# ConvFFN up and gate chunks as 2x2 block products by Strassen's algorithm

## The chip, the cores and the metric

The kernel runs on one core of a Trainium2 chip, in one launch. The metric is the device time of one execution in microseconds (us). The engines are TensorE (PE; PEld is its weight load), VectorE (DVE), ScalarE (ACT), GpSimd (POOL) and SyncE (SP), which here issues most DMAs. Tiles live in SBUF, results of TensorE in PSUM.

## The reference

Two layers of a decoder trunk work on 592 tokens: 16 learned meta tokens, 64 sample tokens (8 sequences of 8) and 512 prompt tokens. Layer 0 has mLSTM and retention heads as its mixer, layer 1 HGRN2; behind each mixer stands a causal ConvFFN. The change touches the ConvFFN alone. With model width 1024, inner width 2816 and a convolution of three taps it is

```python
def conv_ffn(xn, w_in, conv_w, conv_b, w_out, buf):
    t = xn.shape[1]
    u, gate = jnp.split(xn @ w_in, 2, axis=-1)
    padded = jnp.concatenate([buf, u], axis=1)
    conv = conv_b + sum(padded[:, j:j + t] * conv_w[j] for j in range(3))
    h = jax.nn.silu(conv) * gate
    return h @ w_out, padded[:, t:]
# in each layer: x = x + conv_ffn(rms_norm(x, norm_ffn[layer]), ...)
```

All inputs and outputs are f32. Beside the tokens the mixers' states and the last two rows of `u` of each sequence are returned.

## The kernel before

Features lie on partitions, tokens on columns. The residual is 8 chunks `x[c]` of 128 features by 592 tokens. Every f32 matrix product is made of three products of fp32r operands, with each operand split into a rounded part `hi` and a rest `lo`: hi by hi, hi by lo, lo by hi. The residual is split after its gain, before the norm: `gained` makes `h` and `xl` of each chunk, and the factor 1 / rms of each token (`rb`, the same on all partitions) is multiplied in when a result is read out of PSUM.

Weights come in tiles of 128 x 8 x 128 (one output chunk of 128 features for all 1024 inputs, 512 KB). `weights` (lines 296 to 312) issues the DMA into a raw tile `wr` (two slots), ScalarE casts it to `wh` (line 308, three slots), VectorE subtracts to `wl` (line 310, three slots). `stream` (278 to 294) keeps two such tiles fetched ahead of the block at work.

In the ConvFFN there are 22 blocks `in_block(fc)` a layer, one for each chunk of 128 inner features. A block takes the up tile and the gate tile: `dense` (316 on) issues for each of 8 input chunks and 3 terms two matmuls, one for each half of the tokens (296 columns in layer 0, 288 and 290 in layer 1), first for up into one PSUM tile `dp`, then for gate into another. All matmuls are recorded under line 123. Then VectorE reads the results out of PSUM, multiplied by `rb`: up into `ub` (lines 514 and 524), gate into `gt` (line 491). Around `ub` GpSimd does the small copies of the convolution's state (517 to 526). The convolution is one ScalarE pass and two VectorE passes over `cv` (493, 495), then Silu (497), two products with the gate (501, 502) and the split of the result into `bh` and `bl` (505, 506). These are the operands of the output products.

The blocks stand in the order fc 0 to 7, the output products of chunks 0 to 6, fc 8 to 14, those of 7 to 13, fc 15 to 21, those of 14 to 21. VectorE adds the output products to the residual (line 424). Block 0 carries the norm of the residual as hooks: `norm_rows` and `norm_bcast` (274 copies `rb` out of PSUM) run while its products are made.

Other lines that the prediction uses for durations: 225 (squares on GpSimd), 1135 and 1209 (GpSimd in the HGRN2 mixer), 1230 (VectorE there), 1368 (the final norm's products on GpSimd). Each engine takes its instructions in the order that the framework's scheduler wrote down when the kernel was built; there is no reordering on the chip.

## Time and profile before

| | |
|---|---|
| time, median of 3 runs | 1633.36 us (1633.0 to 1635.6) |
| span of the profiled execution | 1633.1 us |
| TensorE busy | 1584.1 us, 13508 matmuls |
| VectorE busy | 938.8 us |
| ScalarE busy | 625.8 us |
| GpSimd busy | 204.2 us |
| ConvFFN of layer 0, inside (640 to 745 us) | 773 matmuls in 105.00 us |
| ConvFFN of layer 1, inside (1310 to 1440 us) | 981 matmuls in 130.00 us |

The time of an execution is taken on the device; the profile is one execution with the hardware profiler on, and all durations below come from that one. Busy times of an engine are sums over its instructions, as the profiler records them from start to end; successive instructions can overlap by a little, so that a start to the next start is shorter than the duration listed.

### The profile page before, as it was taken

To read this page: it belongs to the slowest core of one execution; us is meant where nothing else is said; L and a number is where in the kernel's file an instruction comes from. 1 tells how busy PE (TensorE), PEld (TensorE's weight loads), DVE (VectorE), ACT (ScalarE), POOL (GpSimd) and SP (SyncE) were. 2 spreads that over 40 slices of the span, in tenths; PEclk is the share of its full clock that TensorE was granted. 3 is DMA by queue.
4 is the path that set the end of the run, shared out by engine and by line. 5 is a ranking of instruction groups with operands and counts; after the bars stand their busy time and mean duration, and the time that the engine had idled before them with its cause. 6 is when DMAs were issued, how large, how long until landed. Compare 5 with 4: busy or idle time off the path is not lost. (4 is left out here: it accounts for less than half of the span.)

```text
span 1633.1 us, 32234 instructions
## 1 busy us (share of the span) xinstructions
PE 1584.1 (97%) x13508; PEld 1538.7 (94%) x13508; DVE 938.8 (57%) x1933; ACT 625.8 (38%) x1114; POOL 204.2 (13%) x402
## 2 busy tenths in 40 slices
PE   4999999999999999999999899999999999999997
PEld 4999999999999999999999798898999999999997
DVE  5576564757553454355546876766675535534565
ACT  3543434334331232233345466564443213322343
POOL 4000000000110110010002525333001101100102
PEclk9999999999999999999999999999999999999998
DMA  4334435433323222322422132223233232223244
GB/s 144 97 94 100 94 89 83 141 95 95 88 73 87 78 81 75 91 78 85 146 74 66 56 102 91 61 95 96 92 101 89 71 93 84 74 85 88 80 120 135
DMA packets 236049, 149.61 MB, mean 92 GB/s; under 512 B 7512, under 2 KB 227416, under 8 KB 235904
## 3 DMA queue, kind: packets, MB, share of 16 engines
q1 hardware_dynamic: 235904, 147.56, 31.9%
q8 instruction: 106, 1.74, 0.4%
q14 instruction: 39, 0.32, 0.1%
HBM read 132.89 MB, written 14.65 MB: 90 GB/s over the span
## 5 line engine op out<-in xcount | busy, mean ns | idle before, releaser
L123 PE MATMUL dp<-h,wh 128*128 128x296 f32 (+2 forms) x2176 | 477.8, 301 | 0.8 <-ACT v_c L661 0.5
L308 ACT CAST wh<-wr 128x1024 fp32r<-128x1024 f32 (+3 forms) x240 | 234.1, 978 | 625.2 <-PE dp L123 485.5
L123 PE MATMUL dp<-xl,wh 128*128 128x296 f32 (+2 forms) x2176 | 472.1, 298 | 0.0
L123 PE MATMUL dp<-h,wl 128*128 128x296 f32 (+2 forms) x2176 | 471.7, 298 | 0.0
L123 PEld LDWEIGHTS dp<-h,wh 128*128 128x128 f32 x2176 | 351.2, 189 | 4.3 <-issue 1.8
L123 PEld LDWEIGHTS dp<-h,wl 128*128 128x128 f32 x2176 | 352.1, 189 | 0.0
L123 PEld LDWEIGHTS dp<-xl,wh 128*128 128x128 f32 x2176 | 351.8, 189 | 0.0
L310 DVE TENSOR_TENSOR wl<-wr,wh 128x1024 fp32r<-128x1024 f32 (+3 forms) x240 | 273.8, 1141 | 76.3 <-ACT wh L308 73.0
L123 PE MATMUL dp<-bh,wh 128*128 128x296 f32 (+2 forms) x832 | 182.8, 300 | 2.0 <-DVE x L424 0.5
L123 PE MATMUL dp<-bh,wl 128*128 128x296 f32 (+2 forms) x832 | 179.7, 297 | 0.0
L123 PE MATMUL dp<-bl,wh 128*128 128x296 f32 (+2 forms) x832 | 179.5, 297 | 0.0
L424 DVE TENSOR_TENSOR x<-x,dp 128x592 f32<-128x592 f32 (+2 forms) x72 | 54.9, 763 | 153.1 <-PE dp L123 153.0
L123 PEld LDWEIGHTS dp<-bh,wh 128*128 128x128 f32 x832 | 134.0, 188 | 5.9 <-ACT wh L308 2.4
L491 DVE TENSOR_TENSOR gt<-dp,rb 128x592 f32<-128x592 f32 (+1 forms) x44 | 33.7, 767 | 179.9 <-PE dp L123 179.8
L123 PEld LDWEIGHTS dp<-bl,wh 128*128 128x128 f32 x832 | 134.4, 188 | 0.0
L123 PEld LDWEIGHTS dp<-bh,wl 128*128 128x128 f32 x832 | 134.2, 188 | 0.0
L123 PE MATMUL tp<-wh,h 128*128 128x256 f32 (+3 forms) x280 | 84.6, 303 | 19.0 <-ACT wh L308 11.8
L123 PE MATMUL tp<-wl,h 128*128 128x256 f32 (+3 forms) x280 | 81.2, 290 | 0.3 <-DVE wl L310 0.3
L123 PE MATMUL tp<-wh,xl 128*128 128x256 f32 (+3 forms) x280 | 79.7, 289 | 1.9 <-DVE xl L216 1.9
L495 DVE SCALAR_TENSOR_TENSOR cv<-ub,vec,cv 128x612 f32<-128x612 f32 (+1 forms) x88 | 74.1, 842 | 1.6
L123 PEld LDWEIGHTS tp<-wh,h 128*128 128x128 f32 (+1 forms) x280 | 52.3, 187 | 24.0 <-ACT wh L308 11.8
L497 ACT ACTIVATE cv<-cv 128x612 f32<-128x612 f32 (+1 forms) x44 | 31.1, 708 | 90.8 <-DVE cv L495 90.8
(425 smaller groups left out, 1933.8 us busy)
## 6 DMA issues: line engine op xcount, KB each, us to landing
wr<-in_w_ffn_in SPq DMA_DIRECT2D x88, 512.0 KB, 3.8
wr<-in_w_in_ab SPq DMA_DIRECT2D x32, 512.0 KB, 7.0
wr<-in_w_in_c SPq DMA_DIRECT2D x32, 512.0 KB, 4.1
wr<-in_w_ffn_out SPq DMA_DIRECT2D x32, 448.0 KB, 3.5
wr<-in_w_ffn_out SPq DMA_DIRECT2D x24, 512.0 KB, 3.8
x<-in_x SPq DMA_DIRECT2D x16, 296.0 KB, 5.1
out_H<-s_s SPq DMA_DIRECT2D x8, 576.0 KB, 2.9
wr<-in_w_out_ab SPq DMA_DIRECT2D x16, 256.0 KB, 2.9
```

The source lines that it names most:

```text
L123: T.matmul(out, lhsT=lhsT, rhs=rhs, **kw)
L308: S.copy(hi, raw)
L310: V.tensor_tensor(out=lo, in0=raw, in1=hi.bitcast(F32), op=ALU.subtract)
L424: V.tensor_tensor(out=x[oc][:, a:b], in0=x[oc][:, a:b], in1=p[:, off + a:off + b], op=ALU.add)
L491: V.tensor_tensor(out=gt[:, h0:], in0=pg[:, off + h0:off + NT], in1=rb[:, h0:], op=ALU.mult)
L495: V.scalar_tensor_tensor(out=cv[:, b0:612], in0=ub[:, b0 + j:612 + j], scalar=cw[j], in1=cv[:, b0:612], op0=ALU.mult, op1=ALU.add)
L497: S.activation(cv[:, b0:612], cv[:, b0:612], AF.Silu)
```

## The change

Blocks fc 0 and 1 of each layer stay as they were. From block 2 on (`NOLD = 2`) the up tile and the gate tile of a chunk are taken together as a 2x2 matrix of blocks: rows up and gate, columns the first and the second 4 input chunks, A11, A12 (up), A21, A22 (gate), each 128 x 4 x 128. The tokens are cut in two halves, so that the normed residual is a 2x2 matrix too: B11, B12 (first 4 chunks, first and second half), B21, B22. Strassen's algorithm in Winograd's form makes the four result blocks of seven block products in place of eight; each product is 4 input chunks by 3 terms, 12 matmuls of 296 columns (layer 0) or 290 (layer 1), so that a block has 84 matmuls where it had 96.

The weights' block sums are four GpSimd additions of 128 x 512 (lines 379 to 382: A21+A22, that plus A11, A21+A11 in place of A21, and the second sum plus A12). Split are now two full tiles, one tile of two sums, and a half tile: 3.5 tiles a block where 2 were. `Split` makes each when it is asked for, and `ahead_step` asks for one of the next block's between two products. Raw tiles have a third slot (`alt`).

The operands of the tokens are made once a layer, while block 1 runs. `prepare` (608 to 633): ScalarE applies the gain, GpSimd multiplies by 1 / rms (613), and B11 (negated) and B21/B22 are split by ScalarE and VectorE. `differences` (634 to 639) makes the T blocks on GpSimd from these in 16 operations of 296 columns. `split_differences` (641 to 650) splits the T blocks, into the slots of `h` and `xl`, which the old form reads until block 1 is done.

Results in a block (`strassen_block`, 652 on): the seven products go into PSUM banks a, c (one tile `ac`), b (`sb`) and d (`sd`), in the order B11, B21, T2, T1, T3, T4, B22. Bank a accumulates over three of them, and ScalarE copies it out to SBUF after each (673, 688, 693). VectorE makes `ub` and `gt` as subtractions with one operand in PSUM (680, 685 and 700 for `ub`, 694 and 697 for `gt`). From there on `activate` (582 to 600) is what the old block had: 586 is the first step of the convolution, 588 the two on VectorE, 590 Silu, 597 the cast to `bh`.

```diff
-    # A block is (load, body): load() emits the weights' DMA and their split, body(w) is a generator.
-    def stream(blocks):
-        ahead = []
-        todo = iter(blocks)
-
...
-    def weights(*views):
-        """views: DRAM [128, k, n]; hi/lo f32r tiles of the same shape"""
-        out = []
-        for v in views:
-            k = v[0].shape[1]
-            n = sum(a.shape[2] for a in v)
-            raw = wp.tile([128, k, n], F32, name="wr", tag="wr", bufs=2)
-            o = 0
-            for a in v:
-                ld.dma_start(out=raw[:, :, o:o + a.shape[2]], in_=a)
-                o += a.shape[2]
-            hi = wp.tile([128, k, n], F32R, name="wh", tag="wh", bufs=3)
-            S.copy(hi, raw)
-            lo = wp.tile([128, k, n], F32R, name="wl", tag="wl", bufs=3)
-            V.tensor_tensor(out=lo, in0=raw, in1=hi.bitcast(F32), op=ALU.subtract)
-            out.append((hi, lo))
-        return out
...
+    class Split:
+        def __init__(self, k, n, src):
+            self.k, self.n, self.src, self.made = k, n, src, None
+
+        def get(self):
+            if self.made is None:
+                src = self.src() if callable(self.src) else self.src
+                hi = wp.tile([128, self.k, self.n], F32R, name="wh", tag="wh", bufs=3)
+                S.copy(hi, src)
+                lo = wp.tile([128, self.k, self.n], F32R, name="wl", tag="wl", bufs=3)
+                V.tensor_tensor(out=lo, in0=src, in1=hi.bitcast(F32), op=ALU.subtract)
+                self.made = (hi, lo)
+            return self.made
...
+
+    def ahead_step():
+
+        if ahead:
+            for sp in ahead[0][0] or ():
+                if sp.made is None:
+                    sp.get()
+                    return
...
+        fetch()
+        while ahead:
+            w, body = ahead.pop(0)
+            fetch()
+            for sp in w or ():
+                if not isinstance(w, Quadrants):
+                    sp.get()
+            n = 0
+            for i, (nw, _) in enumerate(ahead):
+                if isinstance(nw, Quadrants):
+                    if n == 0:
+                        nw.add()
+                        if not isinstance(w, Quadrants):
+                            nw[0].get()
+                            nw[1].get()
+                    break
+                if n >= 2 or isinstance(w, Quadrants):
+                    break
+                for sp in nw or ():
+                    sp.get()
+                    n += 1
+            yield from body(w)
+
...
+    turn = [0]
+
+    def quadrants(v1, v2):
+
+
+        r1, r2 = (raw_weights([v], (turn[0] + i) % 3 == 2) for i, v in enumerate((v1, v2)))
+        turn[0] += 2
+        env = {}
+
+        def sums():
+            s12 = tp.tile([128, 2, 4, 128], F32, name="s12", tag="ve", bufs=2)
+            s4 = tp.tile([128, 4, 128], F32, name="s4", tag="nums", bufs=2)
+            a11, a12, a21, a22 = r1[:, 0:4, :], r1[:, 4:8, :], r2[:, 0:4, :], r2[:, 4:8, :]
+            G.tensor_tensor(out=s12[:, 1], in0=a21, in1=a22, op=ALU.add)
+            G.tensor_tensor(out=s12[:, 0], in0=s12[:, 1], in1=a11, op=ALU.add)
+            G.tensor_tensor(out=a21, in0=a21, in1=a11, op=ALU.add)
+            G.tensor_tensor(out=s4, in0=s12[:, 0], in1=a12, op=ALU.add)
+            env.update(s12=s12.rearrange("p a k n -> p (a k) n"), s4=s4)
+
+        q = Quadrants([Split(8, 128, r1), Split(8, 128, lambda: env["s12"]), Split(8, 128, r2),
+                       Split(4, 128, lambda: env["s4"])])
+        q.sums = sums
+        return q
...
+        def prepare(c):
+
+            g = vec[:, V_NFFN + 8 * l + c:V_NFFN + 8 * l + c + 1]
+            x_ = xn[c] = ap.tile([128, NT], F32, name=f"xn{c}", tag=f"b{'hl'[c % 2]}{4 + c // 2}")
+            S.activation(x_, x[c], AF.Copy, scale=g)
+            G.tensor_tensor(out=x_, in0=x_, in1=state["rb"], op=ALU.mult)
+            if c < 4:
+                if c % 2 == 0:
+                    for i in "hl":
+                        ops["1", i, c // 2] = tp.tile([128, 2, 296], F32R, name=f"b11{i}", tag="gate", bufs=4)
+                hi, lo = (ops["1", i, c // 2][:, c % 2, 0:n] for i in "hl")
+                S.activation(hi, x_[:, h1], AF.Copy, scale=-1.0)
+                V.scalar_tensor_tensor(out=lo, in0=x_[:, h1], scalar=-1.0, in1=hi.bitcast(F32), op0=ALU.mult,
+                                       op1=ALU.subtract)
+                ops["B11", c] = (hi, lo)
+            else:
+                if c % 2 == 0:
+                    ops["2", "h", c // 2] = ap.tile([128, 2, 592], F32R, name="b2h", tag="v", bufs=2)
+                    ops["2", "l", c // 2] = tp.tile([128, 2, 592], F32R, name="b2l", tag="st", bufs=2)
+                hi, lo = (ops["2", i, c // 2][:, c % 2, 0:2 * n] for i in "hl")
+                S.copy(hi, x_[:, a0:NT])
+                V.tensor_tensor(out=lo, in0=x_[:, a0:NT], in1=hi.bitcast(F32), op=ALU.subtract)
+                ops["B21", c - 4] = (hi[:, 0:n], lo[:, 0:n])
+                ops["B22", c - 4] = (hi[:, n:2 * n], lo[:, n:2 * n])
+
+        def differences(c):
+
+            p, q = xn[c], xn[c + 4]
+            G.tensor_tensor(out=p[:, h1], in0=p[:, h1], in1=p[:, h2], op=ALU.subtract)
+            G.tensor_tensor(out=p[:, h2], in0=p[:, h2], in1=q[:, h2], op=ALU.subtract)
+            G.tensor_tensor(out=q[:, h2], in0=p[:, h1], in1=q[:, h2], op=ALU.add)
+            G.tensor_tensor(out=q[:, h1], in0=q[:, h2], in1=q[:, h1], op=ALU.subtract)
+
+        def split_differences():
+            for c in (4, 5, 6, 7, 0, 1, 2, 3):
+                hi = xslot(c, "h", F32R)
+                lo = ap.tile([128, NT], F32R, name=f"xl{c}", tag=f"xl{c}")
+                S.copy(hi[:, 0:2 * n], xn[c][:, a0:NT])
+                V.tensor_tensor(out=lo[:, 0:2 * n], in0=xn[c][:, a0:NT], in1=hi[:, 0:2 * n].bitcast(F32),
+                                op=ALU.subtract)
+                a, b = ("T1", "T3") if c < 4 else ("T4", "T2")
+                ops[a, c % 4] = (hi[:, 0:n], lo[:, 0:n])
+                ops[b, c % 4] = (hi[:, n:2 * n], lo[:, n:2 * n])
...
+            def product(out, split, k0, op, start, stop):
+                hi, lo = split.get()
+                for k in range(4):
+                    xh, xl = ops[op, k]
+                    for i, (ww, xx) in enumerate(((hi, xh), (hi, xl), (lo, xh))):
+                        matmul(out, lhsT=ww[:, k0 + k, :], rhs=xx, start=start and k == 0 and i == 0,
+                               stop=stop and k == 3 and i == 2, skip_group_check=True)
+                    if k % 2:
...
+            def body(w):
+                w.add()
+                w[0].get()
+                w[1].get()
+                ac = mm("ac")
+                a, c = ac[:, 0:n], ac[:, 512:512 + n]
+                cs = tmp("cs", 592)
+                s1, u2, u3 = cs[:, 0:n], cs[:, 296:296 + n], cs[:, 0:n]
+                yield from product(a, w[0], 0, "B11", True, True)
+                S.copy(s1, a)
+                w[2].get()
+                b = px("sb")[:, 0:n]
+                yield from product(b, w[0], 4, "B21", True, True)
+
+                ub, gt = tmp("ub", 614), tmp("gt")
+                ubs = ub[:, 0:100].rearrange("p (s i) -> p s i", i=10)
+                V.tensor_tensor(out=ubs[:, s0:, 2:10], in0=b[:, h0 - a0:80 - a0].rearrange("p (s i) -> p s i", i=8),
+                                in1=s1[:, h0 - a0:80 - a0].rearrange("p (s i) -> p s i", i=8), op=ALU.subtract)
+                if l == 1:
+                    V.tensor_tensor(out=ub[:, 100:102], in0=b[:, 2:4], in1=s1[:, 2:4], op=ALU.subtract)
+                m = a0 + n - P0
+                V.tensor_tensor(out=ub[:, 102:102 + m], in0=b[:, P0 - a0:n], in1=s1[:, P0 - a0:n], op=ALU.subtract)
+                up_edges(fc, ub)
+                yield from product(a, w[1], 0, "T2", False, True)
+                S.copy(u2, a)
+                w[3].get()
+                yield from product(c, w[1], 4, "T1", True, True)
+                ahead_step()
+                yield from product(a, w[2], 0, "T3", False, True)
+                S.copy(u3, a)
+                V.tensor_tensor(out=gt[:, h2], in0=u3, in1=c, op=ALU.subtract)
+                d = px("sd")[:, 0:n]
+                yield from product(d, w[2], 4, "T4", True, True)
+                V.tensor_tensor(out=gt[:, h1], in0=u3, in1=d, op=ALU.subtract)
+                ahead_step()
+                yield from product(c, w[3], 0, "B22", False, True)
+                V.tensor_tensor(out=ub[:, 102 + m:614], in0=c, in1=u2, op=ALU.subtract)
+                up_state(fc, ub)
+                activate(fc, ub, gt)
+
+            return (lambda: quadrants(cols(w_in, fc * 128), cols(w_in, DFF + fc * 128)), body)
...
+        NOLD = 2
...
+                if fc == 1:
+                    hooks = ({k: lambda k=k: prepare(k) for k in range(8)}, {k: lambda k=k: differences(k) for k in range(4)})
...
+                if fc == NOLD - 1:
+                    split_differences()
...
-        blocks = [in_block(fc) for fc in range(8)]
+        block = lambda fc: in_block(fc) if fc < NOLD else strassen_block(fc)
+        blocks = [block(fc) for fc in range(8)]
```

How this moves instructions on the engines is seen in their orders. On ScalarE, one block of layer 0's ConvFFN reads like this before; `wr` is a raw weight tile, `cv` the convolution, `gt` the product with the gate:

```order
L505 CAST bh_4725<-gt 128x592
L308 CAST wh<-wr 128x1024 x2
L493 ACTIVATE cv<-ub,vec 128x612
L497 ACTIVATE cv<-cv 128x612
L505 CAST bh_4857<-gt 128x592
L308 CAST wh<-wr 128x1024 x2
```

And now, from the first weight cast of a block on; `s_...` are tiles of block sums, `cs` takes what is copied out of bank a, and lines 673, 688 and 693 are its three copies:

```order
L288 CAST wh<-wr 128x1024
L586 ACTIVATE cv<-ub,vec 128x612
L673 COPY cs<-ac 128x296
L288 CAST wh<-s_4995 128x512
L590 ACTIVATE cv<-cv 128x612
L688 COPY cs<-ac 128x296
L597 CAST bh_5127<-gt 128x592
L288 CAST wh<-wr 128x1024
L693 COPY cs<-ac 128x296
L288 CAST wh<-s_5135 128x1024
```

The convolution (586), Silu (590) and the cast to `bh` (597) belong to the block before; they stand now between the copies 673 and 688 of the block at work and behind them, each in its turn.

On GpSimd a block of layer 0 before is six small operations on `ub`, on the conv state `cst` and on the state to be returned, `cvo`:

```order
L517 MEMSET ub 128x2
L523 COPY ub<-cst 128x8x2
L519 COPY ub<-ub 128x2
L520 COPY ub<-ub 128x2
L526 COPY cvo<-ub 128x16
L525 COPY cvo<-ub 128x2
```

Now the four sums follow them (379 to 382; the two raw tiles are both called `wr`), which are those of the block after the next:

```order
L554 MEMSET ub 128x2
L558 COPY ub<-cst 128x8x2
L556 COPY ub<-ub 128x2
L557 COPY ub<-ub 128x2
L564 COPY cvo<-ub 128x16
L563 COPY cvo<-ub 128x2
L379 TENSOR_TENSOR s_4853<-wr 128x512
L380 TENSOR_TENSOR s_4853<-s_4853,wr 128x512
L381 TENSOR_TENSOR wr<-wr 128x512
L382 TENSOR_TENSOR s_4854<-s_4853,wr 128x512
```

Each small copy keeps its place behind the sums of the block before and ahead of the next sums.

At the start of layer 0's ConvFFN GpSimd before goes from the mixer's last memset straight to the small operations of block 0:

```order
L1105 MEMSET gate 128x14 x2
L517 MEMSET ub 128x2
L523 COPY ub<-cst 128x8x2
L519 COPY ub<-ub 128x2
L520 COPY ub<-ub 128x2
L526 COPY cvo<-ub 128x16
```

Now, behind those of block 0, it has the eight products by 1 / rms (613, the last two shown; `xn` are the normed chunks) and the differences (636 to 639), with the first sums of block 3 (379, 380) and the small operations of block 1 among them:

```order
L613 TENSOR_TENSOR xn_4430<-xn_4430,rb 128x592
L613 TENSOR_TENSOR xn_4443<-xn_4443,rb 128x592
L554 MEMSET ub 128x2
L558 COPY ub<-cst 128x8x2
L636 TENSOR_TENSOR xn_4358<-xn_4358 128x296
L636 TENSOR_TENSOR xn_4371<-xn_4371 128x296
L637 TENSOR_TENSOR xn_4358<-xn_4358,xn_4406 128x296
L637 TENSOR_TENSOR xn_4371<-xn_4371,xn_4419 128x296
L636 TENSOR_TENSOR xn_4382<-xn_4382 128x296
L636 TENSOR_TENSOR xn_4395<-xn_4395 128x296
L637 TENSOR_TENSOR xn_4382<-xn_4382,xn_4430 128x296
L638 TENSOR_TENSOR xn_4406<-xn_4358,xn_4406 128x296
```

These 24 operations stand ahead of the sums of block 4; the splits of the T blocks on ScalarE and VectorE wait for them.

## Rows read from the trace of the kernel before

**Rows 1.** The page: busy microseconds of each engine, share, instructions.

```profile
span 1633.1 us, 32234 instructions
## 1 busy us (share of the span) xinstructions
PE 1584.1 (97%) x13508; PEld 1538.7 (94%) x13508; DVE 938.8 (57%) x1933; ACT 625.8 (38%) x1114; POOL 204.2 (13%) x402
```

**Rows 2.** Windows in both ConvFFNs: stretch, length, busy by engine, TensorE clock, DMA.

```profile
core 0: us, PE busy (x) PEld busy (x) DVE busy (x) ACT busy (x) POOL busy (x), PEclk, DMA share, GB/s
...
640.00:745.00 105.00, 105.00 (x773) 105.00 (x773) 48.26 (x64) 27.61 (x31) 10.65 (x36) 1.00 0.30 85
1310.00:1440.00 130.00, 130.00 (x981) 129.84 (x980) 62.38 (x92) 35.47 (x41) 10.26 (x21) 1.00 0.30 86
```

**Rows 3.** Chain of waits: start, length, engine, tile, line, count.

```profile
1309.29 134.10 PE dp L123 x1008
```

**Rows 4.** VectorE by form: count, busy us, mean ns, idle before.

```profile
L310 DVE TENSOR_TENSOR wl<-wr,wh 128x1024 fp32r<-128x1024 f32 x172 | 211.3, 1229 | 62.0 <-ACT wh L308 58.9
L495 DVE SCALAR_TENSOR_TENSOR cv<-ub,vec,cv 128x612 f32<-128x612 f32 x44 | 37.5, 853 | 0.8
...
L502 DVE TENSOR_TENSOR gt<-gt,cv 128x512 f32<-128x512 f32 x44 | 30.1, 685 | 0.0
...
L310 DVE TENSOR_TENSOR wl<-wr,wh 128x512 fp32r<-128x512 f32 x32 | 21.9, 685 | 2.6 <-ACT wh L308 2.5
...
L506 DVE TENSOR_TENSOR bl<-gt,bh 128x592 fp32r<-128x592 f32 x22 | 17.1, 775 | 15.8 <-ACT bh L505 15.8
...
L424 DVE TENSOR_TENSOR x<-x,dq 128x320 f32<-128x320 f32 x8 | 3.8, 483 | 0.7 <-PE dq L123 0.7
```

**Rows 5.** ScalarE by form, same columns.

```profile
L308 ACT CAST wh<-wr 128x1024 fp32r<-128x1024 f32 x172 | 180.3, 1049 | 431.6 <-PE dp L123 322.4 <-issue 67.2 <-DMA wr<-in_w_in_ab 19.6
...
L493 ACT ACTIVATE cv<-ub,vec 128x612 f32<-128x612 f32 x22 | 19.7, 896 | 0.0
...
L497 ACT ACTIVATE cv<-cv 128x612 f32<-128x612 f32 x22 | 15.8, 716 | 45.5 <-DVE cv L495 45.5
...
L505 ACT CAST bh<-gt 128x592 fp32r<-128x592 f32 x22 | 15.1, 687 | 19.1 <-DVE gt L502 19.1
...
L274 ACT COPY rb<-rbp 128x336 f32<-128x336 f32 x5 | 2.2, 447 | 14.0 <-PE rbp L123 14.0
...
L274 ACT COPY rb<-rbp 128x256 f32<-128x256 f32 x4 | 1.6, 392 | 0.7 <-PE rbp L123 0.7
```

**Rows 6.** GpSimd by form, same columns.

```profile
L1135 POOL TENSOR_TENSOR e<-bl 128x256 f32<-128x256 f32 x16 | 10.4, 647 | 32.1 <-issue 17.4 <-ACT ve L585 8.0 <-DVE sts L1260 4.0
...
L1368 POOL TENSOR_TENSOR y<-y,rb 128x320 f32<-128x320 f32 x8 | 8.7, 1110 | 49.1 <-ACT rb L274 49.1
L1209 POOL TENSOR_TENSOR kd<-bl 128x512 f32<-128x512 f32 x8 | 8.4, 1045 | 0.0
...
L225 POOL TENSOR_TENSOR ssq<-x 128x592 f32<-128x592 f32 x1 | 1.2, 1174 | 17.5 <-DMA x<-in_x 17.5
```

**Rows 7.** Single lines: count, least, median, largest ns.

```profile
L525 POOL COPY cvo<-ub x44: 188/1116/1188, 391.6 to 1561.3; 128x2 f32<-128x2 f32 x44
...
L1368 POOL TENSOR_TENSOR y<-y,rb x8: 858/874/1868, 1611.6 to 1619.4; 128x320 f32<-128x320 f32 x8
...
L1230 DVE TENSOR_TENSOR kd<-kd,bh x8: 759/1198/1247, 900.6 to 1081.6; 128x592 f32<-128x592 f32 x8
```

**Rows 8.** Timeline in a ConvFFN block: start, length, engine, line.

```profile
425.13 0.68 DVE L524 TENSOR_TENSOR ub<-dp,rb 128x512 f32<-128x512 f32 x1
...
425.28 0.19 POOL L519 COPY ub<-ub 128x2 f32<-128x2 f32 x1 [11.16 <-DVE ub L514]
...
425.73 1.22 DVE L310 TENSOR_TENSOR wl<-wr,wh 128x1024 fp32r<-128x1024 f32 x1
...
425.88 1.11 POOL L525 COPY cvo<-ub 128x2 f32<-128x2 f32 x1
```

**Rows 9.** The page, DMA issues: KB each, median us to landing.

```profile
wr<-in_w_ffn_in SPq DMA_DIRECT2D x88, 512.0 KB, 3.8
```

**Rows 10.** Windows again, the kernel's last 7 us, columns as rows 2.

```profile
1626.00:1633.00 7.00, 0.64 (x3) 0.34 (x2) 3.22 (x8) 0.00 (x0) 0.00 (x0) 0.50 0.44 150
```

More of the change, by code (lines that the diff above doesn't have):

```diff
@@ L536, in ffn @@
[L536 removed]
+        blocks += out(0, 7, None, False) + [block(fc) for fc in range(8, 15)]
+        blocks += out(7, 14, None, False) + [block(fc) for fc in range(15, 22)]
         blocks += out(14, 22, next_gain, True, None, spans)
```

131 lines of the change are left out of this document (82 added, 49 removed).

## The prediction

> **What bounds the kernel now.** I read the page's busy table first: TensorE is busy for 97% of a span of 1633.1 us, VectorE for 57% [rows 1]. The chain of waits says the same of the stretch that the change touches: 134.10 us of it are one unbroken run of 1008 dense matmuls [rows 3]. So in the ConvFFN time is the number of matmuls times their pitch, and everything else is hidden as long as it stays hidden. The pitch comes from two stretches inside the ConvFFN, taken by windows: 105.00 us hold 773 matmuls in layer 0 (0.1358 us each) and 130.00 us hold 981 in layer 1 (0.1325 us), at granted clock 1.00 [rows 2]. VectorE is busy 46 to 48% and GpSimd 8 to 10% there, which looks like much room. The groups by form give the durations of what is added [rows 4 to 6], and two further views show what VectorE and GpSimd do to each other [rows 7, 8].
>
> **Matmuls removed.** An old block is 96 matmuls (8 chunks, 3 split terms, 2 halves, 2 results): 13.04 us in layer 0, 12.72 us in layer 1. A new one is 7 products of 12, so 84: 11.41 us at 296 columns; at 290 columns I take 0.1329 us (between the two pitches), 11.16 us. Twenty blocks a layer: 20 x 1.63 + 20 x 1.56 = 63.8 us less. With all else hidden the span would be 1569.3 us.
>
> **Work added in a block.** ScalarE and VectorE split 3.5 weight tiles where they split 2: 1.5 x 1.05 = 1.6 us more on ScalarE, 1.23 + 0.69 = 1.9 us more on VectorE [rows 4, 5]. ScalarE also copies 296 columns out of PSUM three times (0.42 us each, between the 256- and 336-column copies; the former is shown at 0.39). VectorE's subtractions that read PSUM replace as much work that read it before. GpSimd gets four additions of 512 columns. None of this size stands in the trace with two full operands: the 512-column difference has a broadcast operand and takes 1.05 us, the 320-column product of two full tiles takes 0.87 us undisturbed, which by width is 1.40 us [rows 6, 7]. I take 1.18 us, twice the step of 256 columns less its start, and keep 1.05 and 1.40.
>
> By busy time alone that fits: VectorE some 9.7 us, ScalarE 7.5 us, GpSimd 5.4 us, against 11.4 us of TensorE. The rows say that it doesn't. GpSimd's copy of two columns takes 188 ns when alone but 1116 ns in the median [rows 7]. The timeline shows why [rows 8]: other small copies run at 0.19 us while VectorE works on an operand from PSUM, but this one starts just after VectorE's 1.22 us weight subtraction, whose two inputs are both in SBUF, and ends with it. GpSimd's 320-column product goes from 858 to 1868 ns and VectorE's 592-column product from 759 to 1247 ns in the same way [rows 7]. So I take it that a VectorE operation on two SBUF operands and a GpSimd operation that reads SBUF go one after the other.
>
> The Trainium skill (SBUF — State Buffer, Who interferes with whom) says so of both directions and for the whole instruction, and it leaves VectorE's PSUM readers free; it speaks against putting the sums on GpSimd beside VectorE's splits. The trace agrees as far as rows 7 and 8 reach; if the two engines merely shared bandwidth, the first rival below would hold.
>
> In turns a block needs: VectorE's SBUF-only work 3 x 1.23 + 0.69 + 2 x 0.85 + 0.69 + 0.24 (the narrow piece, an estimate) + 0.78 = 7.8 us listed, about 7.1 us counted from start to start (0.60 where 0.68 is listed in rows 8), GpSimd 4 x 1.18 + 0.7 = 5.4 us. That is 12.5 us, already more than TensorE's 11.4.
>
> **What that delays.** The order on ScalarE decides it. The third product of a block accumulates in bank a, then T1 and T3 follow, and T1 waits for the second copy of a (line 688). On ScalarE that copy stands behind Silu of the block before (line 590), and Silu waits for VectorE's second conv step (line 588). Let 0 be the end of the last product of block i-1 in layer 0. VectorE's last subtraction takes until 0.6, ScalarE's weight copy until 1.0 and the first conv step there until 1.8 (0.90), VectorE's weight subtraction from 1.1 to 2.2. The sums can start when their second weight tile has landed, 3.8 us [rows 9] after the split of the first tile of the block before frees its slot, some 2 us ahead of 0: so at about 2. Then they take turns: sum to 3.4, conv step to 4.1, sum to 5.3, conv step to 6.2. Silu 0.72 to 7.0, copy 0.42 to 7.4. TensorE has 12 + 12 + 12 + 4 matmuls before T1, 5.4 us: it stands 2.0 us.
>
> The second wait comes late in the block. The last product overwrites bank c, which VectorE's gate subtraction (line 694) must have read. That stands behind the first weight split of the next block, this behind the bh copy, and this behind the products with Silu, which take turns with sums three and four: Silu 7.0, the narrow split and the fourth sum to 9.1, the two products to 10.2, bh to 11.0, weight copy to 12.0, weight subtraction to 13.2, gate subtraction to 13.6. TensorE would be there at 7.4 + 32 x 0.1358 = 11.8: another 1.9 us. If the weight tile lands 1 us later the conv steps slip ahead of the sums, the first wait goes and the second is 2.9 us. So 2.9 to 3.9 us a block, 2.2 with sums of 1.05 us; I take 3.2 (keeping 0.3, where nothing takes turns, and 4.8, for sums of 1.40). The sums of a block are made during the block before, except for the first two of a group, which fall under the output products: 4 + 5 + 5 = 14 such blocks a layer. 28 x 3.2 = 89.6 us. The five undisturbed blocks a layer lose some 0.3 us each to the same gate wait: 2.7 us.
>
> **The start in each layer.** From 1 / rms on, GpSimd does one small copy, 8 products of 592 columns (between 1.17, a square of one tile [rows 6], and 0.87 / 320 x 592 = 1.6; I take 1.35), 16 differences of 296 columns (0.72; 0.65 is the 256-column one), the four sums of block 3 among them, and small copies: 10.8 + 11.5 + 4.7 + 0.8 = 27.8 us. VectorE's SBUF-only work up to the last T operand is two weight splits, two conv steps, the gate products, one bl, four B11 parts (about 0.45), four B21/B22 parts and five T parts: some 14.7 us. In turns that is up to 42.5 us, by my laying out of both queues 39 to 40, since some of VectorE's parts fall where GpSimd has ended. TensorE has 96 + 24 matmuls to cover it, 16.3 us, and T1 and the gate wait add about 3. I take 27 us a layer, 54 us in all; bounds 14 (GpSimd's queue alone, less the cover) and 33. TensorE stands for more than 10 us there, and where it stood so at the end of the kernel its granted clock was 0.50 [rows 10]: 4 us for the first products of both starts (0 to 10).
>
> Sum: 1633.1 - 63.8 + 89.6 + 2.7 + 54 + 4 = 1719.6 us. The profiled execution's span is 0.3 us below the median of 1633.36 us, so I forecast 1720 us for the median.
>
> The Trainium skill (GPSIMD Engine Reference, Elementwise — side-by-side cycle accounting) measures 4497 ns for a 2048-column addition on GpSimd, by which a sum would be an estimated 1.12 us. No row here has that operation; the forecast by it would be about 1713 us, so it changes nothing that counts.
>
> **Rivals.** First, the sums do not hold VectorE up: its operations keep 1.23 and 0.85 us beside them. Against it stand rows 7 and 8; for it, that they show short or broadcast operations on GpSimd. Then only GpSimd's own queue at the start remains: 1569.3 + 2 x 17 (14, and 3 for T1 and the gate wait) + 38 x 0.3 = 1615 us, faster. It decides from the point where VectorE's weight subtraction stays under 1.3 us while a sum runs. Second, turns are taken but the block order absorbs them, so that a block with sums costs only the 12.5 us of the shared turns: 1569.3 + 54 + 28 x 1.1 + 3 = 1657 us. For it: waits move operations apart and later blocks may settle in a better phase; against it: ScalarE's and VectorE's orders are fixed. Third, TensorE's granted clock falls in the disturbed blocks. Matmuls at 0.8 of the clock cost 28 x 11.3 x 0.25 = 79 us more, 1799 us; against it, gaps of 2 to 3 us between 4 us of matmuls are short beside the stretch at 0.50 [rows 10].
>
> **How the numbers follow.** The forecast has 0.62 (its own range 1675 to 1760: 2.2 to 4.2 us a block and 20 to 30 us a start), the first rival 0.13, the second 0.17, the third 0.05; 0.03 is left for a result near the old time, where start and disturbance are both half as dear. A range of 1625 to 1765 leaves out the first and third rivals. A difference of 0.2% (3.3 us) is what can be told from none: faster 0.14, same 0.04, slower 0.82.
>
> **What would show it.** In the changed profile the matmul count falls by 480, while TensorE's busy share falls well below 97%. VectorE's weight subtractions and conv steps have a maximum or a mean well over 1.23 and 0.85 us, GpSimd's sums run over 1.18 us, and both are undisturbed in the blocks without sums. TensorE's idle time before T1 ends with ScalarE's second copy (line 688), before the last product with VectorE's gate subtraction (line 694). Each layer has one gap of some 20 us behind the second block, ended by the split of the T operands. If the weight subtractions keep their 1.23 us, I am wrong at the root; if they stretch and TensorE still has no gaps in a block, I am wrong on the order.

## The result and the profile after

| | before | with the change |
|---|---|---|
| median | 1633.18 us (1631.98 to 1635.6, 4 runs) | 1737.15 us (1732.16 to 1739.0, 4 runs) |
| ratio to before | 1 | 1.063, interval 1.0611 to 1.0649 |
| profiled span | 1633.1 us | 1736.9 us |

The forecast was 1720 us, slower with a chance of 0.82. The page's busy table of the changed kernel answers to [rows 1]:

```profile
span 1736.9 us, 32105 instructions
## 1 busy us (share of the span) xinstructions
PE 1560.5 (90%) x13028; PEld 1494.8 (86%) x13028; DVE 1176.4 (68%) x2125; ACT 756.8 (44%) x1362; POOL 514.5 (30%) x610
```

480 matmuls fewer, TensorE 97 to 90% busy: it stands idle for 176.4 us of the span (1736.9 less 1560.5) where it stood 49.0. VectorE has 238 us and GpSimd 310 us more. The windows inside the two ConvFFNs answer to [rows 2]:

```profile
core 0: us, PE busy (x) PEld busy (x) DVE busy (x) ACT busy (x) POOL busy (x), PEclk, DMA share, GB/s
640.00:745.00 105.00, 99.31 (x715) 97.39 (x716) 64.67 (x77) 38.16 (x52) 34.07 (x43) 1.00 0.28 82
1310.00:1440.00 130.00, 118.95 (x851) 115.34 (x849) 87.22 (x108) 49.54 (x71) 46.52 (x42) 0.99 0.27 78
```

TensorE idles for 5.7 us of the first stretch and 11.1 of the second, at a granted clock of 1.00 and 0.99. GpSimd went from 10 to 34 and 47 us. Counted in matmuls the loss is larger than this idle time: 715 in place of 773 in the first stretch, 851 in place of 981 in the second, which at [rows 2]'s pitches is 7.9 and 17.2 us of work. Three lines by least, median and largest duration in ns, as in [rows 7]:

```profile
L379 POOL TENSOR_TENSOR s<-wr x40: 1272/1750/2279, 391.1 to 1644.8; 128x512 f32<-128x512 f32 x40
...
L382 POOL TENSOR_TENSOR s<-s,wr x40: 1258/1738/1849, 396.2 to 1650.4; 128x512 f32<-128x512 f32 x40
...
L588 DVE SCALAR_TENSOR_TENSOR cv<-ub,vec,cv x88: 824/1750/2057, 395.1 to 1672.3; 128x612 f32<-128x612 f32 x44, 128x592 f32<-128x592 f32 x44
```

A sum takes 1.26 us when nothing is beside it (the least) and 1.74 in the median. The conv step (L588, line 495 before) is at 0.82 us at least (0.85 in the mean in [rows 4]), and at 1.75 in the median. Two groups of VectorE by form, as in [rows 4]:

```profile
L290 DVE TENSOR_TENSOR wl<-wr,wh 128x1024 fp32r<-128x1024 f32 x172 | 217.6, 1265 | 113.7 <-ACT wh L288 110.7
...
L290 DVE TENSOR_TENSOR wl<-s,wh 128x512 fp32r<-128x512 f32 x40 | 58.0, 1449 | 0.0
```

The 512-column split of a sum went to 1.45 us where the same width took 0.685, but the full weight split is at 1.27, where it was at 1.23. The timeline of one block shows why; here VectorE, GpSimd, ScalarE and TensorE one after the other, each row with start, length, engine and line, and what ended an idle time in brackets:

```profile
727.36 1.23 DVE L290 TENSOR_TENSOR wl<-wr,wh 128x1024 fp32r<-128x1024 f32 x1 [0.24 <-ACT wh L288]
728.50 3.69 DVE L588 SCALAR_TENSOR_TENSOR cv<-ub,vec,cv 128x612 f32<-128x612 f32 x2
732.11 1.75 DVE L290 TENSOR_TENSOR wl<-s,wh 128x512 fp32r<-128x512 f32 x1
733.78 0.23 DVE L680 TENSOR_TENSOR ub<-sb,cs 128x80 f32<-128x80 f32 x1
733.93 1.18 DVE L593 TENSOR_TENSOR gt<-gt,cv 128x80 f32<-128x80 f32 x1
735.03 0.72 DVE L594 TENSOR_TENSOR gt<-gt,cv 128x512 f32<-128x512 f32 x1
...
738.60 0.46 DVE L694 TENSOR_TENSOR gt<-cs,ac 128x296 f32<-128x296 f32 x1
...
741.05 0.47 DVE L700 TENSOR_TENSOR ub<-ac,cs 128x296 f32<-128x296 f32 x1 [0.49 <-PE ac L123]
...
727.92 1.81 POOL L379 TENSOR_TENSOR s<-wr 128x512 f32<-128x512 f32 x1 [0.55 <-DMA wr<-in_w_ffn_in]
729.81 1.73 POOL L380 TENSOR_TENSOR s<-s,wr 128x512 f32<-128x512 f32 x1
731.49 1.82 POOL L381 TENSOR_TENSOR wr<-wr 128x512 f32<-128x512 f32 x1
733.27 1.74 POOL L382 TENSOR_TENSOR s<-s,wr 128x512 f32<-128x512 f32 x1
...
732.22 0.71 ACT L590 ACTIVATE cv<-cv 128x612 f32<-128x612 f32 x1 [2.12 <-DVE cv L588]
732.84 0.39 ACT L688 COPY cs<-ac 128x296 f32<-128x296 f32 x1
...
739.11 0.40 PE L123 MATMUL ac<-b2h,wh 128*128 128x296 f32 x1 [1.20 <-DVE gt L694]
```

The four sums follow one another from 727.92 to 735.0. In that stretch VectorE makes two conv steps in 3.69 us (alone 2 x 0.85), a 512-column split in 1.75 (0.685) and an 80-column product in 1.18 (0.24). The subtraction at 733.78, which reads PSUM, keeps 0.23. When the sums have ended, the 512-column product is back at 0.72. Silu (732.22) and the copy of line 688 behind it (732.84) are late by that. The full weight split (727.36) keeps its 1.23 us since it has begun before the first sum is issued (727.92): there the sum waits for the split and takes 1.81. What TensorE waited for in all (wait, total us, times, longest):

```profile
PE ac L123 <- ACT cs L688: 41.4, 25, 2.6
PE ac L123 <- DVE ub L577: 27.8, 2, 13.9
PE ac L123 <- DVE gt L694: 26.1, 23, 1.2
PE sd L123 <- ACT wh L288: 20.8, 2, 11.6
```

The first and third rows are the two waits inside the blocks, 1.66 us (25 times) and 1.13 us (23 times); the other two are one gap each in each layer's start. From one bh cast (line 597) to the next a block with sums takes 14.78 us in layer 0 (from 606.92 to 621.73, 636.51 and 651.29), 14.64 in layer 1. In layer 0's second group the block behind them, without sums, takes 10.89 and the next 12.86. The first group of each layer is less even, 13.8 to 16.9 us a block with sums.

### The profile page after: what moved, and what is told of

The parts are those of the page before. It is cut to its first block, busy times and chain, and to the rows that moved or that the text cites. A ratio compares the mean times of both kernels' runs of the same rounds, so it can differ in the third digit from the quotient of the medians.

```text
span 1736.9 us, 32105 instructions
## 1 busy us (share of the span) xinstructions
PE 1560.5 (90%) x13028; PEld 1494.8 (86%) x13028; DVE 1176.4 (68%) x2125; ACT 756.8 (44%) x1362; POOL 514.5 (30%) x610
## 5 line engine op out<-in xcount | busy, mean ns | idle before, releaser
L123 PE MATMUL dp<-h,wh 128*128 128x296 f32 (+2 forms) x896 | 200.6, 305 | 0.9 <-ACT v_c L862 0.5
L123 PE MATMUL dp<-h,wl 128*128 128x296 f32 (+2 forms) x896 | 194.9, 298 | 0.0
L123 PE MATMUL dp<-xl,wh 128*128 128x296 f32 (+2 forms) x896 | 194.8, 298 | 0.0
L123 PE MATMUL ac<-h,wh 128*128 128x296 f32 (+1 forms) x480 | 150.6, 314 | 43.0 <-ACT cs L688 41.4
L123 PEld LDWEIGHTS dp<-h,wh 128*128 128x128 f32 x896 | 143.5, 189 | 4.7 <-issue 1.8
L123 PE MATMUL ac<-xl,wh 128*128 128x296 f32 (+1 forms) x480 | 145.9, 304 | 0.0
L123 PE MATMUL ac<-h,wl 128*128 128x296 f32 (+1 forms) x480 | 145.9, 304 | 0.0
L123 PEld LDWEIGHTS dp<-h,wl 128*128 128x128 f32 x896 | 145.2, 188 | 0.0
L123 PEld LDWEIGHTS dp<-xl,wh 128*128 128x128 f32 x896 | 145.0, 188 | 0.0
L588 DVE SCALAR_TENSOR_TENSOR cv<-ub,vec,cv 128x612 f32<-128x612 f32 (+1 forms) x88 | 127.6, 1450 | 5.5 <-ACT cv L586 4.2
L290 DVE TENSOR_TENSOR wl<-s,wh 128x1024 fp32r<-128x1024 f32 x80 | 108.7, 1358 | 4.0 <-ACT wh L288 3.7
```

The source lines that it names most:

```text
L123: T.matmul(out, lhsT=lhsT, rhs=rhs, **kw)
L290: V.tensor_tensor(out=lo, in0=src, in1=hi.bitcast(F32), op=ALU.subtract)
L588: V.scalar_tensor_tensor(out=cv[:, b0:612], in0=ub[:, b0 + j:612 + j], scalar=cw[j], in1=cv[:, b0:612], op0=ALU.mult, op1=ALU.add)
```

## The experiments

**Sums left out**

```diff
-            G.tensor_tensor(out=s12[:, 1], in0=a21, in1=a22, op=ALU.add)
...
+            s12, s4 = turn[2], turn[3]
```

> The four block sums of the weights are left out: the splits that read them read two constant tiles instead, so the ConvFFN's results are not the reference's; every other instruction stays. Theory (VectorE's operations on two SBUF operands and GpSimd's sums go one after the other, and the delay reaches T1 over Silu and line 688): the 28 blocks that stand 14.8 us apart now go to 11.4 + 0.3 = 11.7 us, 3.1 us less each, and each start loses the 4.7 us of sums that lie in its turns, 2 x 4 us: 1737 - 87 - 8 = 1642 us. The second convolution steps fall from 1.45 us in the mean to 0.85. Rival (the sums are innocent; the 1.5 additional weight splits and ScalarE's order delay Silu): T1's wait on line 688 stays, 1725 to 1740 us.

Measured: 1631.53 us, ratio to before 0.9985 (0.9975 to 0.9995). The conv steps are at 0.846 us in the median, T1 has no wait on line 688 left, and a block takes 11.87 us in layer 0. The time is 10 us under the theory's, since TensorE's gaps in the starts shrank by 20.6 us (the two first ones from 27.8 to 19.5 in all, the two second ones from 20.8 to 8.5), where it counted 8. The rival falls: the sums cause the waits inside the blocks. The time also says that without them the change would gain next to nothing, since its starts eat what the matmuls save.

**Sums on VectorE**

```diff
-            G.tensor_tensor(out=s12[:, 1], in0=a21, in1=a22, op=ALU.add)
+            V.tensor_tensor(out=s12[:, 1], in0=a21, in1=a22, op=ALU.add)
...
```

> The four sums on VectorE instead of GpSimd, nothing else. Theory of turns: a sum costs 0.69 us on VectorE instead of 1.26 us in its turns with GpSimd; VectorE has 9.7 + 2.7 = 12.4 us of work a block, which now bounds it at about 12.6 us instead of 14.8: 1737 - 28 x 2.2 - 4 for the starts = 1671 us. Rival (GpSimd's sums run beside VectorE and only VectorE's own length counts): 2.7 us more on VectorE ahead of Silu in each of 28 blocks, 1737 + 76 = 1813 us.

Measured: 1652.61 us, 1.011 (1.0085 to 1.0135). The other three sums moved in the same way. A block takes 12.45 us in layer 0, a sum 0.685 us in the median. Moving work onto the engine that looked busier made the kernel 84.5 us faster: a sum on GpSimd costs VectorE about 1.0 us (two of them make two conv steps 2.0 us longer in the timeline above), more than making it.

**Banks a and c as two tiles**

```diff
-                ac = mm("ac")
-                a, c = ac[:, 0:n], ac[:, 512:512 + n]
+                a, c = px("sa")[:, 0:n], px("sc")[:, 0:n]
```

> PSUM banks a and c as two tiles of their own instead of two halves of one tile; sums stay on GpSimd. T1 writes bank c and needs nothing of bank a; in the program built so, the wait for the copy of line 688 moves from T1 to T3, 12 matmuls or 1.63 us later. Theory (ScalarE's order and this wait decide what the turns cost): the first wait, 1.6 us, is covered, the gate wait of 1.2 us stays or grows to 1.6; a block of 14.8 us goes to 13.2 to 13.5 us: 1737 - 28 x 1.4 = 1698 us. Rival (the turns of VectorE and GpSimd bound the block by their sum, wherever TensorE waits): the waits move to line 694 and the block stays within 0.5 us of 14.8: 1723 to 1737 us.

Measured: 1735.41 us, 1.0623 (1.0607 to 1.0639), blocks of 15.0 us. My theory fell. T1's wait on line 688 had no operand behind it, since that copy reads bank a and T1 writes bank c; it stood there because both were one tile, and it went with the two tiles. What TensorE waits for instead (lines are one less than in the changed kernel):

```profile
PE sc L123 <- DVE gt L693: 51.6, 26, 2.3
...
PE sa L123 <- ACT cs L687: 11.6, 16, 1.6
```

The last product waits 2.0 us (26 times) for VectorE's gate subtraction. Behind some of these longer waits the granted clock fell (0.66 in the 5 us from 590 and from 620), but the two blocks without that, 14.96 and 14.93 us, aren't shorter than the change's either, with VectorE's order in a block the same. So T1's wait on line 688 was a place where time showed, not what sets the block. The time is the rival's; whether the turns bound the block by their sum, or a loop does, is told further down by the run that copies bank c.

**The start's products and differences on VectorE**

```diff
-            G.tensor_tensor(out=x_, in0=x_, in1=state["rb"], op=ALU.mult)
+            V.tensor_tensor(out=x_, in0=x_, in1=state["rb"], op=ALU.mult)
...
-            G.tensor_tensor(out=p[:, h1], in0=p[:, h1], in1=p[:, h2], op=ALU.subtract)
+            V.tensor_tensor(out=p[:, h1], in0=p[:, h1], in1=p[:, h2], op=ALU.subtract)
```

> The eight products by 1 / rms and the sixteen differences of a layer's start on VectorE instead of GpSimd; sums stay on GpSimd. Theory of turns: GpSimd's 24 operations (26 us as they ran) go, VectorE gets 8 x 0.77 + 16 x 0.45 = 13.4 us; both starts (25.4 and 23.1 us of TensorE's idle time in two gaps each) get some 9 us shorter, and TensorE's clock some 2 us back: 1737 - 20 = 1717 us; blocks with sums stay at 14.8 us. Rival (VectorE's own queue sets the start, GpSimd ran beside it): 2 x 10 us longer, 1757 us.

Measured: 1719.08 us, 1.0532 (1.0505 to 1.0559), as the theory said; in layer 0 the blocks with sums stay at 14.8 to 15.2 us but for the first (16.8).

After these the theory was a closed loop: gate subtraction (694), the last product, VectorE's read of it (700), the conv steps in turns with the sums, Silu, gate products, bl, a weight split, and the next gate subtraction, which stands behind all that on VectorE. Two runs lengthen VectorE by one PSUM read, once in the loop and once beside it.

**A gate subtraction twice, in the loop**

```diff
                 V.tensor_tensor(out=gt[:, h2], in0=u3, in1=c, op=ALU.subtract)
+                V.tensor_tensor(out=gt[:, h2], in0=u3, in1=c, op=ALU.subtract)
```

> The gate subtraction of line 694 is made twice, one after the other, with the same operands; all orders stay as they are. It reads PSUM, and from start to start it takes 0.37 us. Theory (a closed loop bounds the block: gate subtraction, last product, line 700, conv steps in turns with the sums, Silu, gate products, bl, weight split, gate subtraction): this operation is in the loop, each of 28 blocks gets 0.37 us longer, 1737 + 10 = 1747 us. Rival (only operations on two SBUF operands take turns with GpSimd, and a block lasts as long as these turns): an operation that reads PSUM costs nothing, 1737 us.

Measured: 1742.58 us, 1.0666 (1.065 to 1.0681).

**The other gate subtraction twice, beside the loop**

```diff
                 V.tensor_tensor(out=gt[:, h1], in0=u3, in1=d, op=ALU.subtract)
+                V.tensor_tensor(out=gt[:, h1], in0=u3, in1=d, op=ALU.subtract)
```

> The counterpart: the other gate subtraction, line 697, is made twice, also from PSUM, also 0.37 us. It stands between line 694 and the next weight split, while the last product runs, and VectorE idles 0.49 us ahead of line 700. Theory of the loop: the idle time takes it up, 1737 us (1735 to 1740). Rival (the block lasts as long as VectorE's whole queue and the sums together, 9.7 + 4 x 1.26 = 14.7 us): every operation on VectorE counts, 1737 + 10 = 1747 us.

Measured: 1736.12 us, 1.0625 (1.0609 to 1.0641). The second costs nothing, as forecast: a PSUM read beside the loop is taken up, and the rival of that run, that VectorE's whole queue counts, falls. Behind the start its blocks keep the change's order on VectorE.

The first costs 5.4 us, half of what was forecast and just clear of the interval, but it isn't the test that it was meant to be, for the orders did not stay: when the kernel was built with one operation more, the framework's scheduler wrote others down. In layer 0's first group ScalarE makes the copy of line 688 ahead of Silu, where the change makes it behind:

```profile
495.98 0.41 ACT L688 COPY cs<-ac 128x296 f32<-128x296 f32 x1 [1.47 <-PE ac L123]
498.61 0.72 ACT L590 ACTIVATE cv<-cv 128x612 f32<-128x612 f32 x1 [2.23 <-DVE cv L588]
```

VectorE has the 512-column split between the two conv steps and bl behind the weight split, and these blocks take 13.5 to 13.7 us. In layer 0's second group line 685 stands ahead of the products with Silu, and blocks take 15.6 to 16.4. So the 5.4 us hold an added operation and changed orders, and say neither whether there is a loop nor how long it is. They do show what order can do: in this one kernel the same operations take 2 us a block more or less (part of that in stretches at a lower clock, 0.66 from 630 to 635). What tests the loop is the next run.

**Bank c copied by ScalarE**

```diff
+                a, c = px("sa")[:, 0:n], px("sc")[:, 0:n]
...
                 yield from product(c, w[1], 4, "T1", True, True)
+                S.copy(gt[:, h2], c)
...
-                V.tensor_tensor(out=gt[:, h2], in0=u3, in1=c, op=ALU.subtract)
+                V.tensor_tensor(out=gt[:, h2], in0=u3, in1=gt[:, h2], op=ALU.subtract)
```

> Banks a and c as two tiles, and ScalarE copies bank c to SBUF behind T1, so that the last product waits for that copy and no longer for VectorE's gate subtraction; the subtraction then has two SBUF operands. Sums stay on GpSimd. Theory of the loop: it now runs over ScalarE's copy, which stands behind the bh cast and one weight cast, some 1.3 us ahead of where VectorE's subtraction ended; a block goes from 14.8 to 13.6 us: 1737 - 28 x 1.2 = 1703 us. Rival (VectorE's queue and the sums bound the block by their sum, whatever waits): 1735 to 1745 us, since the subtraction joins the turns.

Measured: 1671.21 us, 1.0226 (1.0209 to 1.0243), so 66 us less than the change with GpSimd's work untouched; the two tiles alone had given less than 2. VectorE's order in a block is the change's in the second and third group of both layers, so what differs is what the last product waits for: the loop was what set the block, and opening it is worth twice what I forecast. Blocks there take 12.4 to 13.1 us. Its timeline, VectorE and then GpSimd:

```profile
605.11 0.45 DVE L700 TENSOR_TENSOR ub<-sc,cs 128x296 f32<-128x296 f32 x1
605.49 1.21 DVE L290 TENSOR_TENSOR wl<-wr,wh 128x1024 fp32r<-128x1024 f32 x1
606.62 1.75 DVE L588 SCALAR_TENSOR_TENSOR cv<-ub,vec,cv 128x612 f32<-128x612 f32 x2
608.28 1.78 DVE L290 TENSOR_TENSOR wl<-s,wh 128x512 fp32r<-128x512 f32 x1
...
607.93 1.58 POOL L379 TENSOR_TENSOR s<-wr 128x512 f32<-128x512 f32 x1 [4.05 <-DMA wr<-in_w_ffn_in]
```

The conv steps now run undisturbed (two in 1.75 us), because line 700 is no longer late and comes ahead of the sums, which wait for their weights (607.93). VectorE is idle for some 0.5 us of a block here; its own work and the sums in turns fill it.

**All on VectorE, four old blocks**

With the edits of the two runs that moved work to VectorE:

```diff
-        NOLD = 2
+        NOLD = 4
...
+                    hooks = ({k: lambda k=k: prepare(k // 2) for k in (0, 2, 4, 6)}, {k: lambda k=k: prepare(4 + k // 2) for k in (0, 2, 4, 6)})
+                if fc == 2:
+                    hooks = ({2 * k: lambda k=k: differences(k) for k in range(4)}, None)
```

> Sums, products by 1 / rms and differences all on VectorE, and four blocks of the old form in each layer instead of two, over which the preparation is spread. Theory (turns with GpSimd cost the blocks, and the start costs what VectorE's preparation exceeds its idle time in the old blocks by): blocks with sums 12.45 us as with sums on VectorE, others 11.3 us, starts 12 us in all: 1616 us. Rival (the start's price is the splits of the T operands behind the last old block, which more old blocks do not cover): 13 us a layer as now, and four Strassen blocks fewer gain less: 1635 to 1645 us.

Measured: 1619.98 us, 0.9916 (0.9902 to 0.9931): 0.8% faster than before. The gaps of 9 to 14 us in the starts are gone, the longest wait there is 2.1 us.

**That and bank c copied**

The edits of the last two runs together.

> Everything on VectorE and four old blocks as in the run before, and banks a and c as two tiles with bank c copied by ScalarE. Theory of the loop: it no longer holds the blocks, VectorE's queue does with 8.6 + 4 x 0.61 = 11.0 us from start to start, so TensorE bounds them again: 24 blocks with sums go from 12.45 to some 11.6 us, 1620 - 24 x 0.8 = 1600 us. Rival (VectorE's busy time of 12.4 us a block is the bound): no gain, 1617 to 1622 us.

Measured: 1594.37 us, 0.9756 (0.9734 to 0.9777), the fastest. Its bh casts in layer 0:

```profile
566.36 0.69 ACT L597 CAST bh<-gt 128x592 fp32r<-128x592 f32 x1 [0.95 <-DVE gt L594]
...
577.82 0.69 ACT L597 CAST bh<-gt 128x592 fp32r<-128x592 f32 x1 [0.95 <-DVE gt L594]
```

11.46 us here and 11.43 in the next block with sums, against 84 x 0.1358 = 11.41 us of matmuls: TensorE bounds the ConvFFN again.

**Three old blocks, the last one's gate in another order**

```diff
-        NOLD = 4
+        NOLD = 3
...
+        ks = ks or list(range(nk))
+        for k in ks:
...
+  dense(ww[1:2], acts_x(), c0, hooks[1], None, [4, 5, 6, 7, 0, 1, 2, 3] if fc == NOLD - 1 else None)
```

> As the other kernel of this call, with three old blocks instead of four, and the last of them taking its input chunks in the order 4 to 7, 0 to 3 for the gate, so that the slots of the first T operands come free earlier. Theory (a start costs what VectorE's preparation exceeds its idle time by): VectorE has some 18 us of preparation, 12 us of its own and the first sums, 32 us, for the 26 us of two blocks: 6 us a layer more, less 1.4 us for one more Strassen block: 9 us slower than the other kernel of this call, 1609 us. Rival (the preparation is hidden either way, one more Strassen block a layer is a gain): 3 us faster, 1597 us.

Measured: 1601.17 us, 0.9805 (0.9782 to 0.9828), 6.8 us slower than with four, near the 9 that the theory of the start gave (it costs what VectorE's preparation exceeds its spare time by).

**The fastest with its sums on GpSimd**

```diff
-            V.tensor_tensor(out=s12[:, 1], in0=a21, in1=a22, op=ALU.add)
+            G.tensor_tensor(out=s12[:, 1], in0=a21, in1=a22, op=ALU.add)
...
```

> The fastest kernel so far (four old blocks, preparation on VectorE, bank c copied by ScalarE; blocks of 11.43 us) with the four sums back on GpSimd. Theory (a sum on GpSimd holds VectorE up for its whole 1.26 us and VectorE's queue then bounds the block at 12.6 us, as where bank c was copied with the sums on GpSimd): 24 blocks x 1.2 us = 28 us more, 1594 + 28 = 1622 us. Rival (once the loop is open, sums on GpSimd cost nothing, since VectorE's own queue of 8.6 us leaves room for them): 1594 to 1600 us.

Measured: 1630.88 us, 0.998 (0.9968 to 0.9992). The rival falls: 36.5 us for the place of the sums alone. Its bh casts in layer 0:

```profile
566.80 0.69 ACT L597 CAST bh<-gt 128x592 fp32r<-128x592 f32 x1 [2.55 <-DVE gt L594]
...
579.29 0.69 ACT L597 CAST bh<-gt 128x592 fp32r<-128x592 f32 x1 [2.55 <-DVE gt L594]
```

12.49 us a block, 1.06 more than with the sums on VectorE, or 25 us in 24 blocks. Another 9 us are in the starts: the last two old blocks take 33.6 and 32.9 us in the two layers where they took 28.7 and 28.4, since sums stand beside VectorE's preparation there.

**The change with its start alone mended**

```diff
-        NOLD = 2
+        NOLD = 4
...
+            V.tensor_tensor(out=x_, in0=x_, in1=state["rb"], op=ALU.mult)
...
+            V.tensor_tensor(out=p[:, h1], in0=p[:, h1], in1=p[:, h2], op=ALU.subtract)
```

> The changed kernel with its start alone mended: four old blocks in each layer, preparation on VectorE; sums on GpSimd and banks a and c in one tile as in the change. Theory (the starts cost some 33 us a layer, with the two dear blocks fc 2 and 3 among it, and the blocks with sums stay at 14.8 us): 1737 - 66 = 1671 us. By the prediction's own terms, 54 us of starts and 4 us of clock, it would be 1737 - 58 - 4 x 1.6 = 1673 us less what fc 2 and 3 lose by turns. Rival (the start is hidden or paid in any case, the 28 blocks hold the whole loss): above 1700 us.

Measured: 1682.98 us, 1.0302 (1.0285 to 1.032): 54 us less than the change, its blocks still at 14.6 to 15.1 us in the second and third groups. Both losses are real and stand apart, but the start is worth 12 us less than I had put it here.

## Why the prediction was right, and where it was not

It held in time (1720 against 1737 us), in sign and in its first cause.

*Matmuls.* 63.8 us less was right: where nothing holds it, a block takes 11.43 us, and 11.41 was worked out.

*One after the other.* This is shown. A sum was taken at 1.18 us and is 1.26 undisturbed. The trace of the change agrees with the rule that the prediction cited from the Trainium skill (SBUF — State Buffer, Who interferes with whom): in the timeline above conv steps and sums take turns, each step with about 1.0 us of a sum's 1.26 in it, and PSUM reads keep their time. And with the sums gone or on VectorE the median conv step is back at 0.846 us.

*The blocks.* 3.2 us a block was forecast. A block with sums takes 14.78 where its matmuls take 11.41, so 3.4, and in layer 1 14.64 against 11.16, so 3.5. T1's wait was worked out at 2.0 us and the last product's at 1.9; the trace has 1.66 and 1.13, and each costs some 0.27 us more than is listed as idle (from 737.61, the last matmul ahead of the wait of 1.20, to 739.35, the second behind it, are 1.74 us for two pitches of 0.136). Of the blocks without sums the sum counts five a layer, where 20 less 14 are six; that is less than 1 us.

*The step that failed* is the sentence "The order on ScalarE decides it". With T1's wait taken away the time stayed (1735 us), and with the last product's wait on VectorE taken away it fell to 1671. What decides is a loop from the gate subtraction over the last product and VectorE's queue back to the gate subtraction. I had worked out both waits along one path and added them; the first one only takes up slack that the second would show. That 3.2 us came so near to 3.4 is therefore in part luck. The prediction's second rival, that a block costs the shared turns of 12.5 us, describes the block once this loop is open (12.4 to 13.1 us measured). It had a chance of 0.17, with "ScalarE's and VectorE's orders are fixed" against it: true of one build, but what closed the loop was one PSUM bank that VectorE had to read before TensorE could go on.

*The weight splits.* I had written that if they keep 1.23 us I am wrong at the root. They are at 1.27 in the mean, and the root was right: when the sums' second weight tile has landed the block's full split has begun, so it is the first sum that waits (727.36 and 727.92 above). The test named the wrong operation; conv steps and the split of the fourth sum were the ones that wait for sums.

*The start.* 27 us a layer were forecast, as one gap. TensorE's two large gaps are 13.8 + 11.6 in layer 0 and 13.9 + 9.2 us in layer 1, 48.5 against 54. Rows of GpSimd, VectorE, ScalarE and TensorE in layer 0's start:

```profile
398.17 13.32 POOL L613 TENSOR_TENSOR xn<-xn,rb 128x592 f32<-128x592 f32 x8
...
403.28 4.98 DVE L620 SCALAR_TENSOR_TENSOR b11l<-xn,b11h 128x296 fp32r<-128x296 f32 x3
408.19 2.01 DVE L629 TENSOR_TENSOR b2l<-xn,b2h 128x592 fp32r<-128x592 f32 x1
...
416.50 2.67 DVE L629 TENSOR_TENSOR b2l<-xn,b2h 128x592 fp32r<-128x592 f32 x2
...
419.10 0.68 DVE L577 TENSOR_TENSOR ub<-dp,rb 128x512 f32<-128x512 f32 x1
...
435.27 0.68 ACT L645 CAST h<-xn 128x592 fp32r<-128x592 f32 x1 [1.51 <-POOL xn L639]
435.86 1.04 ACT L288 CAST wh<-wr 128x1024 fp32r<-128x1024 f32 x1
...
419.92 0.58 PE L123 MATMUL ac<-b11h,wh 128*128 128x296 f32 x1 [13.83 <-DVE ub L577]
...
436.95 0.61 PE L123 MATMUL sd<-h,wh 128*128 128x296 f32 x1 [11.63 <-ACT wh L288]
...
461.78 0.61 PE L123 MATMUL ac<-b11h,wh 128*128 128x296 f32 x1 [2.12 <-ACT wh L288]
```

GpSimd's eight products take 13.32 us in turns with VectorE's B11 and B21 splits, 1.66 each where 1.35 was taken. VectorE's read of block 1's up product (line 577), which frees the PSUM tile that B11's product needs, stands behind the last of these splits (416.50): that is the first gap, which I had not seen. The second, ahead of T4, is the one that I had forecast, but for its end: not a T operand's split ends it but a weight cast (435.86) that stands on ScalarE behind the last cast of a T operand (435.27), and this one waits for GpSimd's differences.

*The clock.* Its term was mis-sized: 4 us (0 to 10) against some 15. Windows of 5 us, columns as above:

```profile
418.00:423.00 5.00, 3.08 (x12) 3.11 (x13) 2.48 (x3) 0.69 (x1) 5.00 (x6) 0.50 0.00 0
...
438.00:443.00 5.00, 4.44 (x18) 4.44 (x19) 4.87 (x8) 1.12 (x4) 0.09 (x2) 0.50 0.20 57
443.00:448.00 5.00, 5.00 (x33) 5.00 (x33) 2.94 (x6) 2.85 (x5) 0.62 (x5) 0.84 0.18 51
448.00:453.00 5.00, 5.00 (x37) 4.82 (x36) 4.04 (x6) 3.10 (x5) 1.46 (x2) 1.00 0.37 105
...
458.00:463.00 5.00, 2.52 (x15) 1.92 (x13) 3.83 (x8) 3.60 (x5) 2.39 (x6) 0.87 0.00 0
463.00:468.00 5.00, 4.96 (x20) 4.96 (x21) 2.33 (x4) 0.94 (x1) 0.19 (x1) 0.50 0.40 110
```

Around both gaps the granted clock is 0.50 to 0.84, and it falls again in the wait of only 2.12 us ahead of 461.78 (the matmul there takes 0.61 us, as the first ones behind the gaps do), and stays at 0.50 through 463 to 468, where TensorE is busy for 4.96 us. Counted over windows of 10 us, from 420 to 450 us 90 matmuls took 17.6 us where 90 x 0.1358 is 12.2, from 460 to 480 us 78 took 15.2 for 10.6, in layer 1 from 1285 to 1315 us 99 took 18.0 for 13.2: 5.4 + 4.6 + 4.9 us. With 1633.1 - 63.8 + 28 x 3.4 + 48.5 + 15 the sum is 1728 us; the 9 us left are the smaller waits in the starts (listed at 3.3 us in layer 0 and 5.2 in layer 1). Of the 17 us between forecast and span the clock is 11, and these waits, less the 2.7 us of gate waits in the sum, are the rest: blocks 5.6 us dearer and starts 5.5 us cheaper than forecast cancel, which is luck.

The first rival (no hold-up, 1615 us) falls with the runs on the sums, the third (clock down in the blocks) with the clock of 1.00 and 0.99 in the blocks' windows; in a few places it did fall there (0.66 from 475 to 480).

## What to carry to other kernels

Before moving elementwise work onto an idle GpSimd, count its time into VectorE's queue wherever VectorE then works on operands that are all in SBUF: here a sum of 1.26 us there cost more than one of 0.69 us on VectorE itself. Then look for a loop through the matmul engine (a PSUM bank that a busy queue must read before the next product), since one short copy by a third engine opened it and was worth 66 us. And count what has to be prepared before a cheaper form can start, and spread it over as many old blocks as its engine has room in: with four old blocks in place of two, all of it on VectorE, and that copy, the same algorithm is 2.4% faster than before instead of 6.3% slower. Compare the engines' orders before you read a run with one operation more: the scheduler can write others down, and here that changed a block by more than the operation did.
